# A tiled softmax on one core: the store of the first tile moves from Pool's DMA queue to SP's

## The chip, the core and the metric

The kernel runs on one core of one Trainium2 chip. The core has several engines, each with its own instruction stream: VectorE (DVE), ScalarE (ACT), GpSimd (POOL), SyncE (SP) and TensorE (PE, unused here). Data moves between the chip's memory and the core's on-chip memory by 16 DMA engines, which all DMA queues share. In this kernel three streams issue DMAs: SP, Pool and ACT. A DMA that one of them issues is cut into packets, and each of the 16 DMA engines moves a share of them.

The metric is the time of one execution in microseconds (us), as the device measures it. The changed kernel is compared with the kernel before.

## What is computed

The input `x` is a float32 array of 32 x 512 x 1024, 67.1 MB, and the temperature is 0.5. The output is the softmax over the last axis of `x / temperature`, in the same shape and type:

```python
def reference(x, temperature):
    scaled = x / temperature
    shifted = scaled - np.max(scaled, axis=-1, keepdims=True)
    exp_x = np.exp(shifted)
    return (exp_x / np.sum(exp_x, axis=-1, keepdims=True)).astype(np.float32)
```

All of `x` has to be read once and an output of the same size written once, 134.2 MB together.

## The kernel before

The 16,384 rows of 1024 numbers are cut into 11 tiles, which the code calls passes (`PASSES`, line 10). A tile has 128 partitions, and each partition holds 11, 12 or 9 whole rows: the first tile has 11 (5,632 KB), the next nine have 12 (6,144 KB each), the last has 9 (4,608 KB). Each tile is worked on in groups of rows, the numbers in `PASSES`: 4, 4 and 3 for the first tile, 6 and 6 for the next nine, 4, 3 and 2 for the last.

Only four tiles fit on chip at once (`BUFS = 4`, line 11). A tile is loaded, turned into its softmax in place and stored from the same buffer. Tile i + 4 reuses the buffer of tile i, so load i + 4 can't start before store i has landed.

For each group the work is:

- `maximum` (lines 63 to 72): DVE reduces each row to its maximum (line 69) and scales it into a bias (line 72).
- `exponential` (lines 74 to 85): ACT computes the exponential row by row, with that bias, and sums each row as it goes (line 78).
- `divide` (lines 87 to 98): DVE takes the reciprocal of the sums (line 90) and multiplies the rows by it, in one instruction for the group (line 93) or row by row (line 96).
- `store` (lines 100 to 109): after the last group of a tile, the whole tile is written with one DMA (line 108), and the load of the tile four further on is issued (line 60).

The order of instructions is written out by hand (`tc.manual_schedule()`, line 113): four loads first, then for each group its maximum and exponential, and after them the division and the store of the group before (near the end, for the first groups of the last two tiles, the division of the group before comes first). Each engine runs its own part of this order strictly in sequence, and waits where it needs another's result.

Three streams issue the DMAs:

- SP issues all loads (line 60), in the order of the tiles. From the fifth on, each waits for the store that frees its buffer.
- Pool issues the stores of tiles 0 to 5 (`BY_POOL = 6`, line 16). Its queue's descriptors are made by software; the profile calls the queue software_dynamic, q0.
- ACT issues the stores of tiles 6 to 10. The profile calls its queue hardware_dynamic, q10; SP's is hardware_dynamic too, q1.

Before the first store, Pool copies one number per partition out of tile 2 into a small tile named `seen` (line 106). The copy's result is not used. It makes Pool wait until tile 2 has been loaded, so that the store behind it on Pool's stream is not issued earlier.

The document calls the transfers load 0 to load 10 and store 0 to store 10, by tile.

Of the kernel before, what the change touches and what calls it, by code (L numbers as in the profile page):

```python
# [1 line left out]

# [4 lines left out]

PASSES = [[4, 4, 3]] + [[6, 6]] * 9 + [[4, 3, 2]]  # L10
BUFS = 4

WHOLE = (2, 3, 4, 6, 8)


BY_POOL = 6

ALONE = 9


@with_exitstack
def kernel(
    ctx: ExitStack,
    tc: tile.TileContext,
    x: bass.AP,
    temperature: bass.AP,
    out: bass.AP,
):
    nc = tc.nc
    f32 = mybir.dt.float32  # L30
    scale = 1.0 / float(temperature)
    extreme = mybir.AluOpType.max if scale > 0 else mybir.AluOpType.min

    P = 128
    xf = x.flatten_outer_dims()
    of = out.flatten_outer_dims()
    n, d = xf.shape
    rows = [sum(ks) for ks in PASSES]
    assert sum(rows) * P == n

    data = ctx.enter_context(tc.tile_pool(name="data", bufs=BUFS))
    stats = ctx.enter_context(tc.tile_pool(name="stats", bufs=4))


    groups = []
    for i, ks in enumerate(PASSES):
        for j, k in enumerate(ks):
            groups.append((i, sum(ks[:j]), k))

    def dram(t, i):  # L50
        block = t[P * sum(rows[:i]) : P * sum(rows[: i + 1]), :]
        return block.rearrange("(p k) d -> p k d", p=P, k=rows[i])

    tiles, small = [], []

    def load():
        i = len(tiles)
        if i < len(PASSES):
            xt = data.tile([P, rows[i], d], f32, name="xt")
            nc.sync.dma_start(out=xt, in_=dram(xf, i))  # L60
            tiles.append(xt)

    def maximum(g):
        i, a, k = groups[g]
        top, bias, sums, recip = (
            stats.tile([P, k], f32, name=name) for name in ("top", "bias", "sums", "recip")
        )
        small.append((bias, sums, recip))
        nc.vector.tensor_reduce(  # L69
            out=top, in_=tiles[i][:, a : a + k, :], axis=mybir.AxisListType.X, op=extreme  # L70
        )
        nc.vector.tensor_scalar_mul(bias, in0=top, scalar1=-scale)  # L72

    def exponential(g):
        i, a, k = groups[g]
        bias, sums, _ = small[g]
        for b in range(k):
            nc.scalar.activation(  # L78
                tiles[i][:, a + b, :],
                tiles[i][:, a + b, :],  # L80
                mybir.ActivationFunctionType.Exp,
                bias=bias[:, b : b + 1],
                scale=scale,
                accum_out=sums[:, b : b + 1],
            )

    def divide(g):
        i, a, k = groups[g]
        _, sums, recip = small[g]
        nc.vector.reciprocal(recip, sums)  # L90
        if i in WHOLE:
            xt = tiles[i][:, a : a + k, :]
            nc.vector.tensor_mul(xt, xt, recip.unsqueeze(2).to_broadcast([P, k, d]))  # L93
            return
        for b in range(k):
            nc.vector.tensor_scalar_mul(  # L96
                tiles[i][:, a + b, :], in0=tiles[i][:, a + b, :], scalar1=recip[:, b : b + 1]
            )

    def store(g):  # L100
        i, a, k = groups[g]
        if a + k == rows[i]:
            if i == 0:


                nc.gpsimd.tensor_copy(stats.tile([P, 1], f32, name="seen"), tiles[2][:, 0, 0:1])  # L106
            queue = nc.gpsimd if i < BY_POOL else nc.scalar
            queue.dma_start(out=dram(of, i), in_=tiles[i])  # L108
            load()

    with tc.manual_schedule():
        for _ in range(BUFS):
            load()
        for g in range(len(groups) + 1):

            alone = g < len(groups) and groups[g][0] >= ALONE and groups[g][1] == 0
            if g > 0 and alone:
                divide(g - 1)  # L120
                store(g - 1)
            if g < len(groups):
                maximum(g)
                exponential(g)
            if g > 0 and not alone:
                divide(g - 1)
                store(g - 1)


# [1 line left out]
_INS = ['x', 'temperature']  # L131
_OUTS = [((32, 512, 1024), 'float32')]

_NUMBERS = {'temperature': 0.5}


# [26 lines left out]
```

## Time and profile before

| | |
|---|---|
| Median of 3 runs | 317.3 us (317.12 to 318.05) |
| Span of the profiled execution | 316.0 us |
| DVE busy | 257.3 us, 81% of the span |
| ACT busy | 148.4 us, 47% |
| POOL busy | 3.7 us, 1% |
| Read from memory, written to it | 67.11 MB, 67.11 MB |
| Mean rate over the span | 425 GB/s |
| Issue to landing, stores by Pool, 6,144 KB | 36.6 us (median of 5) |
| Issue to landing, stores by ACT, 6,144 KB | 33.1 us (median of 4) |
| Issue to landing, loads by SP, 6,144 KB | 36.4 us (median of 9) |
| Issue to landing, store 0, by Pool, 5,632 KB | 29.2 us |
| Issue to landing, load 0, by SP, 5,632 KB | 15.6 us |

The profile is of one execution; its span runs from the first to the last recorded instruction or transfer, and times within it are counted from its start. The only time that the profile gives for that execution is its span. The runs' times are taken around the whole execution, and their median is 1.3 us longer.

"Issue to landing" is the time from the instruction that issues a DMA until its last byte has arrived. Transfers that are under way together share the 16 DMA engines, and one behind another in its queue waits for it, so these times are not the speed of one transfer.

The page also gives the chain of work that ended last, and the groups of instructions with what each waited for. A line such as "L69 DVE" means an instruction of line 69 on VectorE. A busy row has one digit for each of 40 equal slices of the span, in tenths; 9 is 90% or more.

### The profile page before, as it was taken

The numbers are of one execution on the slowest core, as the hardware profiler recorded it, in microseconds if no ns is written. First come the engines' busy times: TensorE is split into PE (matmuls) and PEld (weight loads), VectorE is DVE, ScalarE is ACT, GpSimd is POOL, SyncE is SP. The second block draws the span as 40 slices with busy tenths as digits, with TensorE's granted clock in tenths as the row PEclk, the third lists the DMA queues.
The fourth block names the chain that finished last, engine by engine and source line by source line (L and its number), as shares of the span: only waits on it lengthen the run. The fifth ranks groups of instructions, "written<-read, shape, count | busy, mean of one in ns | idle before, by whom it ended". The sixth has DMA issues, their size and how long they took to land.

```text
span 316.0 us, 529 instructions
## 1 busy us (share of the span) xinstructions
DVE 257.3 (81%) x150; ACT 148.4 (47%) x257; POOL 3.7 (1%) x11
## 2 busy tenths in 40 slices
DVE  0099999999999699979949993997399999888900
ACT  0048477468174444717181771447154705916600
POOL 0000010000000000000000000000000000000000
DMA  9999999999999999999999999999999999999995
GB/s 365 402 460 398 473 423 370 394 468 396 485 404 411 485 398 429 468 404 454 436 404 473 417 404 479 411 412 473 411 423 460 411 448 420 428 478 417 398 465 238
DMA packets 3171, 134.24 MB, mean 425 GB/s; under 512 B 352, under 2 KB 352, under 8 KB 352
## 3 DMA queue, kind: packets, MB, share of 16 engines
q1 hardware_dynamic: 1584, 67.11, 49.7%
q0 software_dynamic: 864, 37.22, 27.2%
q10 hardware_dynamic: 720, 29.88, 21.9%
q14 instruction: 3, 0.02, 0.0%
HBM read 67.11 MB, written 67.11 MB: 425 GB/s over the span
## 4 chain that ended last, share of the span: by engine, by line
DMA 47%; DVE 29%; ACT 10%; issue 9%; DVEq 0%; SPq 0%; POOLq 0%
DMA xt<-in_x_dram 24%; DMA out_dram<-xt 23%; DVE top L69 17%; ACT xt L78 10%; DVE xt L96 9%; DVE xt L93 2%; DVE bias L72 1%; DVE recip L90 0%; DVEq L158 0%; SPq L60 0%; POOLq L108 0%
## 5 line engine op out<-in xcount | busy, mean ns | idle before, releaser
L78 ACT ACTIVATE xt<-xt,bias 128x1024 f32<-128x1024 f32 x128 | 145.2, 1135 | 134.4 <-DVE recip L90 73.2
L69 DVE TENSOR_REDUCE top<-xt 128x6 f32<-128x6144 f32 (+3 forms) x24 | 140.1, 5836 | 36.9 <-DMA xt<-in_x_dram 36.9
L93 DVE TENSOR_TENSOR xt<-xt,recip 128x6144 f32<-128x6144 f32 x10 | 65.6, 6558 | 0.6 <-DVE recip L90 0.2
L96 DVE TENSOR_SCALAR xt<-xt,recip 128x1024 f32<-128x1024 f32 x68 | 46.3, 749 | 0.5
L78 ACT ACTIVATION_READ_ACCUMULATOR xt<-xt,bias 128x1 f32 x128 | 23.9, 186 | 0.0
L78 ACT ACT_TABLE_LOAD x1 | 1.3, 1283 | 16.4 <-DMA xt<-in_x_dram 16.4
L90 DVE RECIPROCAL recip<-sums 128x6 f32<-128x6 f32 (+3 forms) x24 | 4.3, 181 | 4.8 <-ACT xt L78 4.8
L108 POOL DMA_DIRECT2D out_dram<-xt x6 | 3.3, 555 | 128.9 <-ACT xt L78 83.7
L72 DVE TENSOR_SCALAR bias<-top 128x6 f32<-128x6 f32 (+3 forms) x24 | 4.1, 171 | 0.8
L106 POOL COPY seen<-xt 128x1 f32<-128x1 f32 x1 | 0.2, 185 | 45.0 <-DMA xt<-in_x_dram 45.0
L144 POOL MEMSET const-bfloat16-1.0<- 128x1 bf16 x1 | 0.1, 102 | 0.0
L144 POOL MEMSET const-uint8-127<- 128x1 uint8 x1 | 0.1, 102 | 0.0
L144 POOL MEMSET const-float32-0.0<- 128x1 f32 x1 | 0.1, 99 | 0.2 <-issue 0.2
L144 POOL MEMSET const-float32-1.0<- 128x1 f32 x1 | 0.1, 99 | 0.0
## 6 DMA issues: line engine op xcount, KB each, us to landing
xt<-in_x_dram SPq DMA_DIRECT2D x9, 6144.0 KB, 36.4
out_dram<-xt POOLq DMA_DIRECT2D x5, 6144.0 KB, 36.6
out_dram<-xt ACTq DMA_DIRECT2D x4, 6144.0 KB, 33.1
xt<-in_x_dram SPq DMA_DIRECT2D x1, 5632.0 KB, 15.6
out_dram<-xt POOLq DMA_DIRECT2D x1, 5632.0 KB, 29.2
xt<-in_x_dram SPq DMA_DIRECT2D x1, 4608.0 KB, 36.3
out_dram<-xt ACTq DMA_DIRECT2D x1, 4608.0 KB, 14.1
```

The source lines that it names most:

```text
L69: nc.vector.tensor_reduce(out=top, in_=tiles[i][:, a : a + k, :], axis=mybir.AxisListType.X, op=extreme)
L72: nc.vector.tensor_scalar_mul(bias, in0=top, scalar1=-scale)
L78: nc.scalar.activation(tiles[i][:, a + b, :], tiles[i][:, a + b, :], mybir.ActivationFunctionType.Exp, bias=bias[:, b : b + 1], scale=scal ...
L90: nc.vector.reciprocal(recip, sums)
L93: nc.vector.tensor_mul(xt, xt, recip.unsqueeze(2).to_broadcast([P, k, d]))
L96: nc.vector.tensor_scalar_mul(tiles[i][:, a + b, :], in0=tiles[i][:, a + b, :], scalar1=recip[:, b : b + 1])
L106: nc.gpsimd.tensor_copy(stats.tile([P, 1], f32, name="seen"), tiles[2][:, 0, 0:1])
L108: queue.dma_start(out=dram(of, i), in_=tiles[i])
L144: nc = _bacc.Bacc("TRN2", target_bir_lowering=False, num_devices=1)
```

## The change

One line decides which stream stores a tile. After the change the first tile's store is issued by SP instead of Pool. All other stores and all loads stay with their streams, and the copy into `seen` stays on Pool.

```diff
@@ -104,7 +104,7 @@
                 nc.gpsimd.tensor_copy(stats.tile([P, 1], f32, name="seen"), tiles[2][:, 0, 0:1])
-            queue = nc.gpsimd if i < BY_POOL else nc.scalar
+            queue = nc.sync if i == 0 else nc.gpsimd if i < BY_POOL else nc.scalar
             queue.dma_start(out=dram(of, i), in_=tiles[i])
             load()
```

On SP's stream the store stands behind loads 0 to 3 and ahead of load 4. On Pool's stream the first DMA is now store 1, and the copy into `seen` comes ahead of that. On DVE and ACT every instruction and its place are the same as before.

## The prediction

> **What bounds the kernel now.** I read the page first, its busy slices, its DMA queues and its chain.
>
> ```profile
> span 316.0 us, 529 instructions
> DVE  0099999999999699979949993997399999888900
> DMA  9999999999999999999999999999999999999995
> GB/s 365 402 460 398 473 423 370 394 468 396 485 404 411 485 398 429 468 404 454 436 404 473 417 404 479 411 412 473 411 423 460 411 448 420 428 478 417 398 465 238
> DMA packets 3171, 134.24 MB, mean 425 GB/s; under 512 B 352, under 2 KB 352, under 8 KB 352
> q1 hardware_dynamic: 1584, 67.11, 49.7%
> q0 software_dynamic: 864, 37.22, 27.2%
> q10 hardware_dynamic: 720, 29.88, 21.9%
> ```
>
> The DMA row is at 9 in every slice but the last, while VectorE (DVE) has holes. The kernel is bound by the 16 DMA engines: 134.24 MB in 316.0 us. (The slices' GB/s jump because a packet counts where it starts.) The three queues are SP's loads (q1), Pool's stores (q0) and ACT's stores (q10).
>
> Next I read the work by stretches: start and end, length, busy time of DVE, ACT and POOL, clock, DMA share, GB/s.
>
> ```profile
> 24.00:44.00 20.00, 19.61 (x21) 12.03 (x23) 0.00 (x0) 1.00 1.00 433
> 44.00:64.00 20.00, 19.86 (x16) 13.95 (x26) 0.85 (x2) 1.00 1.03 417
> 84.00:104.00 20.00, 19.86 (x8) 11.80 (x21) 0.53 (x1) 1.00 1.00 433
> 144.00:184.00 40.00, 35.14 (x24) 20.84 (x37) 1.07 (x2) 1.00 1.00 433
> 264.00:300.00 36.00, 31.33 (x34) 24.09 (x42) 0.00 (x0) 1.00 1.00 431
> ```
>
> The rate is 433 GB/s with loads alone (24 to 44), with SP and Pool sharing (84 to 184) and at the end, mostly with ACT alone. One stretch is lower, and cut to one microsecond it shows where:
>
> ```profile
> 48.00:49.00 1.00, 1.00 (x1) 0.58 (x2) 0.00 (x0) 1.00 3.09 786
> 49.00:50.00 1.00, 1.00 (x1) 0.00 (x0) 0.00 (x0) 1.00 0.00 0
> 50.00:51.00 1.00, 0.93 (x4) 0.41 (x1) 0.00 (x0) 1.00 0.00 0
> 51.00:52.00 1.00, 1.00 (x3) 1.00 (x3) 0.00 (x0) 1.00 1.56 676
> ```
>
> Sixteen packets, one to an engine, start between 48 and 49, and none again until after 51. In the trace's packet records a load packet (49,152 bytes) takes 1.815 us from the second tile on; these sixteen took 2.89 to 4.08. Summing packet bytes against the steady rate, the kernel is 2.50 us behind at 44 us (first load's start: first packet at 1.73, slow) and 3.78 us behind at 54, then between 3.63 and 3.79 until the end. So in the whole middle the DMA loses one thing: 1.27 us, just before the first store's packets. Pool's timeline names the neighbours:
>
> ```profile
> 45.46 0.18 POOL L106 COPY seen<-xt 128x1 f32<-128x1 f32 x1 [45.02 <-DMA xt<-in_x_dram]
> 46.04 0.67 POOL L108 DMA_DIRECT2D out_dram<-xt  x1 [0.39 <-issue]
> 65.86 0.53 POOL L108 DMA_DIRECT2D out_dram<-xt  x1 [19.16 <-DVE xt L96]
> ```
>
> Store 0 is issued at 46.04, 2.2 us ahead of the slow packets. It is at once the first store of the run and the first transfer of Pool's queue. That queue never runs empty later: each further store is issued before the one ahead of it has landed. ACT's queue starts at 208.8 and shows no such loss.
>
> **The change part by part.** The instructions are the same but for one: line 108's first DMA goes from Pool's queue to SP's, between load 3 and load 4. A 12-row tile is 8 packets per engine, 8 x 1.815 = 14.5 us alone; the 11-row first tile 8 x 1.665 = 13.3 us alone. Two busy queues alternate packet by packet, as the records from 53 to 69 us show.
>
> Removed: Pool's first DMA (0.67 us on Pool) and its wait behind the copy `seen`. Pool's next instruction, store 1, waits for DVE until 65.6 anyway, so nothing is gained there. As the first of its kind it may take 0.67 in place of 0.53; 0.13 us hidden under store 0's packets, and without that cover still 0.13.
>
> Added on SP: a wait for tile 0's last division (line 96, ends 43.84) and one DMA issue, 0.33 to 0.50 us by the load rows. Queued behind it on SP is load 4 alone, which waited for store 0's landing before too. Cost on SP nothing; the cover is load 3's packets.
>
> Store 0's own transfer: a store issued by SP is not in the trace. By the nearest rows, 45,056-byte packets take 1.665 us on q1 (load 0) and on q0 (store 0), and 49,152-byte ones 1.815 us on q1, q0 and ACT's hardware queue q10. I take the change at nothing; the bounds are in the stall below.
>
> The Trainium skill, in "DMA: Bandwidth & Descriptors" (Specifications and "Issuing engine by pattern"), says a simple store belongs on Sync, whose hardware path is generally faster, with about 0.6 us to the first byte against 1 us in software. Were that on the path, its 0.4 us would give an estimate of 316.9. Equal packet times on the queues above leave me at 317.3.
>
> Order: before, load 3 and store 0 shared the engines; store 0 landed at 46.04 + 29.2 = 75.24, load 3 at 71.4. Now store 0 stands behind load 3 in one ring; the rings keep order (loads 0, 1, 2 landed at 16.35, 30.87, 45.41, about 14.5 apart). Load 3 runs alone from 45.0 to 59.5, 11 us earlier, and gains nothing: DVE is busy until it reaches that tile at 78.9. Store 0 starts at 59.5. Store 1's first packet follows its issue at 65.86 by 1.0 us at the least (load 0: 0.74 to 1.73) and 6.3 at the most (ACT's first store: 208.80 to 215.07); I take 3.8 (load 4, issued at 75.31, first packet 79.08, one other queue busy, as here). So store 0 has the engines alone to 69.7, six of its eight packets; two alternate with store 1, 2 x 3.48 = 7.0, to 76.7, and it lands near 78, some 2.5 us later. Load 4 follows: before, it landed at 108.13; now between that and 111.5, the lower end if store 1 finishes before store 2's packets come. Store 1, which has the engines alone from 76.7 to 81.9, lands near 94 in place of 100.58.
>
> What is late next: pass 4's maximum by up to 3.4 us, and store 3 with it. None of it moves the end by itself, because bytes passed over are moved by the other queue: load 5 is issued when store 1 lands, near 94, some 14 us before load 4 ends (before: 100.64 against 108.13), so a next load always waits. The engines have no gap between 59.5 and the end. Cost 0.
>
> The tail decides whether that holds. Load 8 lands at 226.09 and DVE and ACT run from there to store 10's issue at 300.94; its first packet starts at 302.04, just as the first engine is done with store 9, and the last engine at 303.86. The slack is thus 0 to 1.8 us. Load 8's landing depends on how many store packets pass before it, so it can move by about one packet, 1.8 us, either way. Earlier is free; later costs 0 to 1.8. I take 0: when load 7 lands late, store 6 is issued late too and takes less from load 8.
>
> The stall: bounds -1.27 us (gone) and +1.27 (a second). I take 0: it comes with a queue's or a store's first start, and both still happen.
>
> The same skill page ("Latency and other measured facts") offers, as a best guess, that software descriptor rings load ports that some DMA engines need. The rows agree in part: at Pool's first store all 16 engines lost time, one 2.27 us, though later Pool stores cost none. By the guess the loss goes to Pool's first store wherever that is, an estimate of 317.3 again.
>
> Sum: span 316.0 + 0 (issue) + 0 (order) + 0 (tail) + 0 (stall) = 316.0; the median of the runs, 317.3, lies 1.3 us above the span, which I keep: 317.3 us.
>
> **The rivals.**
> *The stall disappears.* It may need loads and a newly started store queue side by side, or Pool's queue starting under full load traffic. Store 0 now follows load 3 in a running ring, and store 1 starts Pool's queue when only store 0 moves. For it: loads' packets were the slow ones, store 0's own were not, and ACT's first store cost nothing. Against: nothing shows that loads must be there. 317.3 - 1.27 = 316.0.
>
> *Pool's queue pays at each start from empty: slower.* Before, it started once. Now store 1 ends early: at 81.9 it has about three packets left, 3 x 3.63 = 10.9, so it ends near 92.8 and store 2 is issued at 92.89. The point is whether q0 is empty when store 2 arrives; if so, a second 1.27 us falls there: 318.6. For it: the sum puts both within 0.1 us. Against: SP's queue, empty from 71 to 79, and ACT's restarted without loss, and no row shows Pool's.
>
> *The tail idles: slower.* Load 8 lands a packet late, and store 10 is issued up to 1.8 us after the engines run dry: 317.3 + 0.9 to 1.8 = 318.2 to 319.1. Against it speaks the feedback above.
>
> **How the numbers follow.** Forecast, the stall moves or stays: 0.46, 317.3, own range 317.1 to 318.05 (the runs shown). Stall gone: 0.29. Second start: 0.14. Tail: 0.11. No run can tell less than 0.3% (0.95 us) from no change; 1.27 us is over it. So faster 0.29, same 0.46, slower 0.25. The range runs from the lowest run less the stall, 317.12 - 1.27 = 315.85, rounded to 315.8, to 318.7, just over the second start; the far half of the tail's case is left out.
>
> **What would show it.** Right: load 3 landing near 60, store 0 near 78, load 4 at 108 to 111.5, a stretch of 433 GB/s from 45 to 65, and one run of long packets near 66 to 70 (or at 60, if it belongs to the first store). No long packets: first rival. Another group near 93 to 97: second. Store 10's first packet more than 1.1 us behind the end of store 9's: third. I am wrong altogether if a store in SP's queue moves at another rate than 433 GB/s, or if load 5 is issued after load 4 has landed.

## The result, and the profile after

| | before | after |
|---|---|---|
| Median of 4 runs each | 317.31 us (317.12 to 318.05) | 328.24 us (327.62 to 329.63) |
| Ratio, after to before | | 1.034 (95% interval 1.0312 to 1.0369) |
| Span of the profiled execution | 316.0 us | 325.9 us |
| Store 10 issued | 300.94 us | 310.13 us |
| Last packet ended | 314.7 us | 324.3 us |

The change costs 10.9 us by the medians and 9.9 us by the profiled spans. The prediction, no change, was wrong, and its range did not hold the time. The page after, the same lines as before:

```profile
span 325.9 us, 528 instructions
DVE  0099999999999049999979990599599999878900
DMA  9999999999699999999999999999999999999995
GB/s 354 444 392 471 398 465 404 362 451 475 290 380 392 440 428 440 428 363 392 386 380 398 392 452 416 452 411 458 404 458 410 422 418 458 431 418 452 416 430 240
DMA packets 3171, 134.24 MB, mean 412 GB/s; under 512 B 352, under 2 KB 352, under 8 KB 352
q1 hardware_dynamic: 1728, 72.88, 53.8%
q0 software_dynamic: 720, 31.46, 23.0%
q10 hardware_dynamic: 720, 29.88, 21.2%
```

Store 0's 5.77 MB went from q0 to q1, as the change says, and the bytes are the same. New is a 6 in the DMA row, in the eleventh slice (81 to 90 us), with 290 GB/s in the row below. Further on, slices 18 to 23 (139 to 187 us) have DMA at 9 throughout and yet only 363 to 398 GB/s: the engines are busy and move less. The work by stretches (start and end, length, busy time of DVE, ACT and POOL, clock, DMA share, GB/s) puts both in numbers, and the short ones show two places closely:

```profile
24.00:44.00 20.00, 19.61 (x20) 12.03 (x21) 0.00 (x0) 1.00 1.00 433
44.00:64.00 20.00, 19.86 (x17) 13.94 (x25) 0.18 (x1) 1.00 1.01 414
84.00:104.00 20.00, 19.86 (x8) 11.47 (x21) 0.53 (x1) 1.00 0.92 354
144.00:184.00 40.00, 38.03 (x24) 21.07 (x39) 1.06 (x2) 1.00 0.98 379
264.00:300.00 36.00, 32.37 (x23) 17.73 (x31) 0.00 (x0) 1.00 1.00 434
...
57.00:58.00 1.00, 1.00 (x1) 0.83 (x2) 0.00 (x0) 1.00 2.78 786
58.00:59.00 1.00, 1.00 (x1) 0.00 (x0) 0.00 (x0) 1.00 0.00 0
59.00:60.00 1.00, 1.00 (x1) 0.00 (x0) 0.00 (x0) 1.00 0.00 0
60.00:61.00 1.00, 1.00 (x1) 0.00 (x0) 0.00 (x0) 1.00 1.67 721
...
88.00:89.00 1.00, 1.00 (x1) 1.00 (x3) 0.00 (x0) 1.00 0.01 0
89.00:90.00 1.00, 1.00 (x1) 1.00 (x3) 0.00 (x0) 1.00 0.16 49
90.00:91.00 1.00, 1.00 (x1) 1.00 (x3) 0.00 (x0) 1.00 2.42 737
```

From 84 to 104 the rate fell from 433 to 354 GB/s, and near 89 the engines stood empty. From 144 to 184 it fell from 433 to 379 with a DMA share of 0.98: the packets took longer. The loss at the first store is still there, at 57 to 61 in place of 48 to 52.

The prediction's own measure was packet bytes against the steady 433 GB/s. By it the 9.6 us between the last packets' ends come as follows:

| stretch | lost more than before |
|---|---|
| first store's start (45 to 55 before, 55 to 65 after) | -0.3 us |
| 85 to 100 us | +3.9 us |
| 140 to 185 us | +5.2 us |
| everything else, in small parts | +0.8 us, what is left |

The chain of waits names what emptied the engines (start and length in us, what). First before, then after:

```profile
65.86 34.72 DMA out_dram<-xt
100.58 0.02 SPq L60
...
100.64 22.04 DMA xt<-in_x_dram
```

```profile
66.20 22.79 DMA out_dram<-xt
88.98 0.02 SPq L60
89.01 0.03 issue
89.04 29.19 DMA xt<-in_x_dram
118.22 0.02 issue
118.25 6.56 DVE top L69
```

The transfer that begins at 66.20 is store 1, and what it releases at 88.98 is SP. SP's timeline after (start, length, instruction, count) says which loads those are:

```profile
0.74 1.88 SPq L60 DMA_DIRECT2D xt<-in_x_dram  x4
44.20 0.34 SPq L108 DMA_DIRECT2D out_dram<-xt  x1
89.04 38.92 SPq L60 DMA_DIRECT2D xt<-in_x_dram  x3
```

Behind four loads and store 0, the next instruction is load 4, at 89.04. Store 0 had landed at 79.94, so load 4 was not released by store 0. The list of waits of the built programs, which the prediction did not read, says it outright (semaphore names: DMASW0 is Pool's first DMA, DMASW1 its second, DMAHW0 to DMAHW4 the first to fifth DMA of a hardware queue; "xt_129" is load 4, "xt_170" load 5):

```
before
5 L60 DMACopy xt_129<-in_x_dram 128x12288 [waits DMAHW0_49,DMASW0_49,DVE_49]
6 L60 DMACopy xt_170<-in_x_dram 128x12288 [waits DMAHW1_49,DMASW1_49,DVE_49]
after
5 L108 DMACopy out_0_dram<-xt_63 128x11264 [waits DMAHW0_49,DVE_49]
6 L60 DMACopy xt_129<-in_x_dram 128x12288 [waits DMAHW1_49,DMASW0_49,DVE_49]
7 L60 DMACopy xt_170<-in_x_dram 128x12288 [waits DMAHW4_49]
```

Before, load 4 waits for load 0's and store 0's end: it takes tile 0's buffer, and load 5 takes tile 1's. After, load 4 waits for load 1 and for Pool's first DMA, which is now store 1: it takes tile 1's buffer, and load 5, behind it, waits for store 0 and takes tile 0's. The order of the instructions is the predicted one; the tile pool, which hands out the four buffers, gave two of them the other way round. The later tiles follow in turn: tile 8 takes tile 4's buffer, tile 9 tile 5's.

### The profile page after: what moved, and what is told of

Its sections match the earlier page's. It is cut to its first block, busy times and chain, and to the rows that moved or that the text cites. A ratio compares the mean times of both kernels' runs of the same rounds, so it can differ in the third digit from the quotient of the medians.

```text
span 325.9 us, 528 instructions
## 1 busy us (share of the span) xinstructions
DVE 257.2 (79%) x150; ACT 148.4 (46%) x257; POOL 3.2 (1%) x10
## 4 chain that ended last, share of the span: by engine, by line
DMA 44%; DVE 32%; ACT 10%; issue 8%; DVEq 0%; SPq 0%; POOLq 0%
DMA xt<-in_x_dram 26%; DVE top L69 19%; DMA out_dram<-xt 19%; ACT xt L78 10%; DVE xt L96 8%; DVE xt L93 4%; DVE bias L72 1%; DVE recip L90 1%; DVEq L158 0%; SPq L60 0%; POOLq L108 0%
## 5 line engine op out<-in xcount | busy, mean ns | idle before, releaser
L96 DVE TENSOR_SCALAR xt<-xt,recip 128x1024 f32<-128x1024 f32 x68 | 46.3, 747 | 0.5
L108 POOL DMA_DIRECT2D out_dram<-xt x5 | 2.8, 558 | 134.2 <-ACT xt L78 91.2
```

The lines of the kernel that those rows point to most:

```text
L96: nc.vector.tensor_scalar_mul(tiles[i][:, a + b, :], in0=tiles[i][:, a + b, :], scalar1=recip[:, b : b + 1])
```

## Experiments

The first question is whether the buffers or the queue cost the time. Three others came up on the way: whether a store among the loads costs something of its own, what made the packets long from 140 to 185 us, and why moving the store with the old buffers still left 2.3 us. In the recorded texts the letters stand for these: A, the swapped buffers make the loss; P, the order of load and store packets on an engine makes packets long; K, the engines drift apart while two stores alternate; L, load 4 is merely issued late.

### Which buffer, or which queue

Two kernels give tile i buffer i modulo 4 by four pools of one buffer each. The first is the changed kernel, the second the kernel before with the same edit, as a control:

```diff
-    data = ctx.enter_context(tc.tile_pool(name="data", bufs=BUFS))
+    data = [
+        ctx.enter_context(tc.tile_pool(name=f"data{b}", bufs=1)) for b in range(BUFS)
+    ]
...
-            xt = data.tile([P, rows[i], d], f32, name="xt")
+            xt = data[i % BUFS].tile([P, rows[i], d], f32, name="xt")
```

> Store 0 stays on SP, but each tile has a buffer of its own turn (tile i in buffer i mod 4), so load 4 waits for store 0 and load 5 for store 1. Theory A (the loss comes from the swapped buffers, by which load 4 waits for store 1): load 4 is issued near 80 in place of 89, the engines never run dry, 317.3 within 1 us. Theory B (a store in the queue of the loads costs by itself, wherever the buffers are): still 326 to 329.

> The kernel before, with four pools of one buffer each in place of one pool of four; store 0 by Pool. A and B alike: 317.3 within 0.5 us, with load 4 issued near 75. If it differs, the four pools cost something themselves, and the other runs are to be read against this one.

The third leaves store 0 on Pool and swaps the buffers alone, for tiles 4 and 5 and for 8 and 9, which follow them:

```diff
-            xt = data[i % BUFS].tile([P, rows[i], d], f32, name="xt")
+            xt = data[(i ^ 1 if i in (4, 5, 8, 9) else i) % BUFS].tile([P, rows[i], d], f32, name="xt")
```

> Store 0 by Pool as before the change; tiles 4 and 8 take the second buffer and tiles 5 and 9 the first, so load 4 waits for store 1. Theory A: load 4 is issued when store 1 lands, near 89 to 100, the engines run dry before it or shortly after, and the time is 326 to 330. Theory B: 317.3 within 1 us. In between would say that both take part.

| | median (lowest to highest) | ratio to before |
|---|---|---|
| store 0 on SP, buffers in turn | 319.64 us (317.64 to 320.66) | 1.0066 (1.0046 to 1.0085) |
| store 0 on Pool, buffers in turn | 317.32 us (316.95 to 319.53) | 1.0003 (0.9978 to 1.0029) |
| store 0 on Pool, buffers swapped | 328.07 us (327.62 to 328.86) | 1.0343 (1.0322 to 1.0364) |

The third kernel and its control came out as theory A said; the first missed both ranges, by 1.3 us above A's and far below B's. Swapped buffers alone make the whole loss, with store 0 still on Pool. Its stretches and its chain are those of the changed kernel:

```profile
84.00:104.00 20.00, 19.86 (x8) 11.30 (x19) 0.53 (x1) 1.00 0.92 354
144.00:184.00 40.00, 38.83 (x24) 21.89 (x39) 1.07 (x2) 1.00 0.98 377
```

```profile
66.37 22.63 DMA out_dram<-xt
...
89.07 29.52 DMA xt<-in_x_dram
```

With the store on SP and the buffers in turn, both stretches are whole again:

```profile
84.00:104.00 20.00, 19.86 (x8) 11.35 (x19) 0.53 (x1) 1.00 1.00 433
144.00:184.00 40.00, 35.10 (x23) 20.70 (x36) 1.07 (x2) 1.00 1.00 435
```

So 8.6 of the 10.9 us (328.24 - 319.64) go with the buffers. Another 2.3 us (319.64 - 317.31) stay with the store on SP, which neither stretch shows. The two don't add up: the swap alone cost 10.7 us, the store on SP alone 2.3, and both together 10.9. In the changed kernel store 0's engines ended 2.4 us apart, but store 1's only 0.6, at 88.0 to 88.6, just before the engines ran dry.

### What a store in the loads' queue costs by itself

To see whether the 2.3 us belong to SP's queue, store 0 went to ACT's, buffers in turn:

```diff
-            queue = nc.sync if i == 0 else nc.gpsimd if i < BY_POOL else nc.scalar
+            queue = nc.scalar if i == 0 or i >= BY_POOL else nc.gpsimd
```

> Buffers in turn as in the first of these runs, store 0 by ACT, whose queue no other store uses until store 6. Theory A: 317.3 within 1 us, since the buffers alone decide. Theory B (cost of the loads' queue): 317.3 too. A third theory, that the loss at the first store belongs to Pool's queue, expects 316.0 here if ACT's queue starts without loss; the trace of the changed kernel speaks against it, as there the slow packets came ahead of SP's store: 1.0 to 1.3 us are lost again.

It took 322.22 us (319.51 to 323.59), ratio 1.0145 (1.0094 to 1.0197): slower than on SP, and a miss for all three theories. Its stretches near the end show the loss:

```profile
285.00:300.00 15.00, 13.65 (x14) 6.53 (x11) 0.00 (x0) 1.00 0.87 374
300.00:315.00 15.00, 7.19 (x11) 3.88 (x8) 0.00 (x0) 1.00 0.72 311
```

In the kernel before, the same stretches have 419 and 370 GB/s. The packet records tell why. Each of the 16 DMA engines brings its own share of a transfer, and by its end there is a first engine and a last one. The table has the end of the first and of the last engine's share, in us. A transfer lands behind the last: before, load 8 landed at 226.09.

| | store 0 | load 8 | load 10 | last transfer |
|---|---|---|---|---|
| before | 73.6 to 74.9 | 224.1 to 225.7 | 278.5 to 280.3 | 313.0 to 314.7 |
| the change | 77.1 to 79.5 | 224.3 to 235.0 | 285.3 to 289.8 | 321.9 to 324.3 |
| on SP, buffers in turn | 77.0 to 80.1 | 222.1 to 225.9 | 276.5 to 281.8 | 312.9 to 316.3 |
| on ACT, buffers in turn | 76.7 to 79.1 | 218.3 to 232.5 | 275.4 to 287.5 | 319.4 to 320.2 |

On ACT's queue the engines drifted 14.2 us apart by load 8. Those ahead ran out of work near the end, while DVE waited for the share of those behind. On SP's queue the drift is 3 us from store 0 on, and it comes out as a last transfer whose engines end 3.4 us apart. By packet bytes against the steady rate, that kernel was 0.16 us behind the kernel before at 45 us and still 0.16 at 310, so its loss is in the last transfers. That gave a theory, K: the engines drift apart while store 0's and store 1's packets alternate, and the drift costs the time. Its rival, L, was that load 4 is issued late (80.6 against 75.3). Two edits held store 1 back by copies on Pool, one by a little (1 copy), one until store 0 is nearly through (4 copies):

```diff
+            if i == 1:
+                junk = junks.tile([P, 1024], f32, name="junk")
+                for _ in range(4):
+                    nc.gpsimd.tensor_copy(junk, tiles[i][:, rows[i] - 1, 0:1024])
```

> Store 0 by SP, buffers in turn (319.6 so far), with one copy of a row on Pool ahead of store 1, about 1 us. Theory K (the remaining 2.3 us come from the engines drifting apart, which starts when store 1's first packet meets some engines just before and others just after a packet's end, and a transfer lands with its last engine): another start moves the spread, and the time changes by 1 to 3 us either way, with the end following the spread of the last transfers. Rival L (store 0's later landing costs the 2.3 us): 319.6 within 0.5 us, whatever the spread is.

> Store 0 by SP, buffers in turn (319.6), with four copies of a row on Pool ahead of store 1, so that store 1's packets start when store 0's are done and the two never alternate. Theory K: no engine meets store 1 earlier than another in the middle of store 0, the spread stays under 2 us, store 0 lands near 74.5, and the time is 317.0 to 317.8. Theory L expects 317.3 too, since store 0 lands early. If a store in the loads' queue costs something by itself, it stays at 319.6.

With 1 copy store 1 was issued at 67.0 and the time stayed: 319.49 us (319.13 to 320.2), ratio 1.0064 (1.0041 to 1.0086), with store 0's engines again 3.0 us apart. The change that K expected did not come, and the time stayed as L said; but the spread had not changed either, so the run doesn't separate the two. With 4 copies store 1 was issued at 70.07, store 0's engines ended within 73.4 to 74.1, no transfer was ever more than 1.2 us apart, and the median was 317.24 us (nine of the twelve runs from 317.03 to 318.11, three from 319.96 to 322.03), ratio 1.0013 (0.998 to 1.0045). Its stretches:

```profile
84.00:104.00 20.00, 19.86 (x8) 11.63 (x21) 0.53 (x1) 1.00 1.00 433
144.00:184.00 40.00, 35.10 (x23) 20.91 (x37) 1.06 (x2) 1.00 1.00 433
```

So a store in the loads' queue need not cost anything that can be measured, and it brought nothing either: no kernel of this study is faster than the one before.

Load 4 was also earlier there (74.5), so L was not yet out. Two kernels with store 0 on Pool and buffers in turn issued load 4 late by itself, behind copies on Pool that read tile 0. The first kernel had 13 copies of 1024 numbers per partition, the second these:

```diff
+            if i == 1:
+                junk = junks.tile([P, 1024], f32, name="junk")
+                for n in [1024] * 7 + [64]:
+                    nc.gpsimd.tensor_copy(junk[:, 0:n], tiles[0][:, 0, 0:n])
+                load()
+            if i > 0:
+                load()
```

> Store 0 by Pool, buffers in turn (317.3 so far), but load 4 is held until Pool has made 13 copies of a row behind store 1's issue, so that it is issued near 80 in place of 75, as late as where SP stores tile 0. Theory L (the later load 4 costs the 2.3 us by which SP's store of tile 0 with buffers in turn is slower): 319 to 320. Theory K (the engines' drifting apart costs them, and being late by itself is made up by the other queue): 317.3 within 0.8 us, if the spread between the first and the last engine of a transfer stays near 1 to 2 us; slower only if that spread grows.

> As the run in which load 4 is held behind copies on Pool, but with eight copies, the last one short, so that load 4 is issued near 80 and not at 87.5, and the engines don't run dry. Store 0 by Pool, buffers in turn (317.3 without the copies). Theory L (a later load 4 costs the 2.3 us by itself): 319 to 320. Theory K (what costs is the spread between the first and the last engine of a transfer): 317.3 within 0.8 us if the spread stays below 2 us, and up to 320 if it reaches 3 us or more.

With 13 full copies load 4 came at 87.5, later than meant, and the engines ran nearly dry: 321.59 us (319.1 to 323.45), ratio 1.0118 (1.0075 to 1.0161), of which 2.4 us were lost from 85 to 105, and its engines then drifted up to 5.1 us apart. That is another loss than the one in question, both expectations missed, and nothing follows. With 8 copies load 4 came at 81.0, as late as with the store on SP, the engines stayed within 2.1 us, and the time was 317.51 us (316.93 to 319.55), ratio 1.0001 (0.9979 to 1.0023). L falls: a late load 4 by itself costs nothing that can be told. K stands in so far as the 2.3 us went where the drift went. What makes the engines drift isn't shown. That two stores alternate can't be all of it: on ACT's queue store 0 ran beside load 3 first, and the drift grew from 2.4 us there to 14.2 at load 8.

### What made the packets long

From 140 to 185 us of the changed kernel the engines are busy, and a 49,152-byte packet of load 6 or store 3 takes 2.07 or 2.06 us on average, against 1.815. The records don't name the engine of a packet, but packets follow one another closely enough to be strung together. Fifteen of the 16 strings put each load packet ahead of the store packet of the same number, and in most of these pairs one of the two, more often the store's, takes 2.1 to 3.4 us, typically 2.4. In the sixteenth the store is one packet ahead, and all but two of its packets stay at 1.81. Theory P: the order decides, a load's packet with the store's packet of the same place in the transfer behind it. Store 3 was held back by 3, 1 and 2 copies on Pool in the changed kernel:

```diff
+            if i == 3:
+                junk = junks.tile([P, 1024], f32, name="junk")
+                for _ in range(3):
+                    nc.gpsimd.tensor_copy(junk, tiles[i][:, rows[i] - 1, 0:1024])
```

> The changed kernel (store 0 on SP, buffers swapped), with three copies of one row on Pool between tile 3's last division and store 3, so that store 3 starts some us behind load 6 in place of together with it. Theory P (in the changed kernel the 5 us between 140 and 190 are lost because load 6 and store 3 move the same packet numbers side by side, load packet k and then store packet k on each engine): their packets go back to 1.815 us, and 322 to 324.5 remain of 328.2. Rival S (the loss comes from the engines being out of step, or from this stretch as such): 327 to 330.

> The changed kernel with one copy ahead of store 3 (three made 323.8 of 328.2). Theory P in its bare form: if store 3's first packet still comes right behind load 6's first on most engines, the packets beside it stay long and the time is 327 to 329; if it comes a packet later, they are 1.815 us and the time is 323 to 324.5. A rival by which the delay helps in proportion (1 us of 3): about 326.7 whatever the order.

> The same with two copies. Theory P: again one of two times by the order of the first packets, 327 to 329 or 323 to 324.5, and 323 to 324.5 the likelier, as store 3 is issued some 2 us later than in the changed kernel. The rival in proportion: about 325.3.

| copies | store 3 issued | engines with long packets | median | ratio to before |
|---|---|---|---|---|
| 0 (the change) | 132.2 | 15 | 328.24 us | 1.034 (1.0312 to 1.0369) |
| 1 | 133.7 | nearly all | 328.18 us (326.92 to 329.29) | 1.0324 (1.0286 to 1.0361) |
| 2 | 134.2 | 4 | 328.54 us (327.45 to 330.11) | 1.0344 (1.0299 to 1.039) |
| 3 | 135.3 | none | 323.79 us (323.23 to 324.57) | 1.0197 (1.016 to 1.0233) |

With 3 copies, 3.1 us of delay bring 4.5 us back: that stretch is whole and the first loss stays.

```profile
84.00:104.00 20.00, 19.86 (x8) 11.41 (x20) 0.53 (x1) 1.00 0.91 354
144.00:184.00 40.00, 39.79 (x24) 22.32 (x40) 1.07 (x2) 1.00 1.00 431
```

With 2 copies both orders are in one execution. These are two of its strings from 136 us on, L for load 6, S for store 3, with the time of each packet in us:

```
engine A   L1.81 L1.81 S1.81 L1.81 S1.81 L1.81 S1.81 L1.81 S1.81 L1.81 S1.81
engine B   L1.81 S1.81 L1.81 S2.40 L1.81 S2.48 L1.81 S2.44 L1.81 S2.45 L1.81
```

Engine A had two load packets before the store's first, engine B one. They run at the same moments, and only B's store packets are long. Twelve engines went like A, four like B. So the long packets go with the order on each engine, not with the moment. But the time did not fall, and its expectation, 323 to 324.5, missed. Twelve engines were now ahead of four: load 6 ended on them between 162.8 and 169.0, load 8 between 222.7 and 237.1, and those ahead idled at the end, by the stretches:

```profile
144.00:184.00 40.00, 39.79 (x24) 22.31 (x40) 1.06 (x2) 1.00 1.00 420
285.00:300.00 15.00, 12.43 (x13) 6.11 (x11) 0.00 (x0) 1.00 0.86 373
300.00:315.00 15.00, 10.55 (x16) 8.55 (x16) 0.00 (x0) 1.00 0.79 338
```

The middle stretch is nearly whole (420 GB/s) and the tail has what it saved: a loss on four engines cost as much as one on fifteen.

A sharper form of P was that packets of the same place, and so the same partitions, disturb each other. Two kernels wrote store 3 as two DMAs, partitions 64 to 127 first, meant to make the places differ, and then 0 to 63 first as a control:

```diff
-            queue.dma_start(out=dram(of, i), in_=tiles[i])
+            if i == 3:
+                for half in (slice(64, 128), slice(0, 64)):
+                    queue.dma_start(out=dram(of, i)[half], in_=tiles[i][half])
+            else:
+                queue.dma_start(out=dram(of, i), in_=tiles[i])
```

> The changed kernel with store 3 in two transfers, partitions 64 to 127 first and then 0 to 63, so that the store moves the other half of the partitions than the load beside it. Theory P: the long packets between 136 and 169 are gone, 322 to 324.5. Rival S: 327 to 330.

> The control to the run with halves: the changed kernel with store 3 in two transfers, partitions 0 to 63 first. Theory P: the store's first half meets the load's packets of the same partitions on half of the engines only, so 324 to 328, slower than with the upper half first. Rival S: the same as with the upper half first, both 327 to 330. If both are near 323, the second transfer or the other share of partitions per engine is what helps, not the order.

They took 331.53 us (329.25 to 333.07), ratio 1.0433 (1.0372 to 1.0494), and 333.14 us (331.13 to 335.08), ratio 1.0489 (1.0433 to 1.0546), with packets of up to 4.6 us in the first. Both are slower than the change and beyond what P or its rival S had said. So the sharper form has no support, and the order of the halves does not help. As the records don't say which partitions a packet holds, and a store in two parts changes more than the places, they don't rule it out.

The last one tried to bring the slow order about in the kernel before, with buffers in turn, by 7 such copies ahead of store 3:

> Store 0 by Pool, buffers in turn (317.3), with seven copies of a row on Pool ahead of store 3, so that its first packet should follow load 6's first packet on most engines, as in the changed kernel. Theory P in its bare form (a store that starts right behind the first packet of a load, and goes on packet by packet beside it, is slow together with that load): packets of 2 us and more between 131 and 160, and 320 to 324. Rival (the slow packets of the changed kernel need something else of that kernel): packets of 1.815 us and 317.3 to 318.5. If the start misses the step, the trace shows it and nothing follows.

It took 318.1 us (317.34 to 319.17), ratio 1.0017 (0.9995 to 1.0039). Store 3's packets came ahead of load 6's, so the slow order was not reached, and nothing follows.

## Why the prediction was wrong, by its own steps

**What bounds the kernel: right.** The engines' bytes and losses account for the time after as for the time before.

**The step that failed: load 4 behind store 0.** The prediction said "Queued behind it on SP is load 4 alone, which waited for store 0's landing before too", and then "Load 4 follows". It took which store a load waits for from the kernel before, and compared only the order of instructions, in which nothing else moved. In the changed program load 4 waits for store 1. Shown by the waits listed above, by load 4's issue at 89.04, 9.1 us after store 0's landing, and by the kernel that swaps the buffers alone: 328.07 us. The prediction's two signs of being "wrong altogether" missed this: load 5 was issued at 89.42, long before load 4 landed at 118.22, and the store on SP's queue moved at the steady rate (from 65 to 75 us it lost 0.03 us). Its line "load 4 at 108 to 111.5" was the one that showed it.

**"The engines have no gap between 59.5 and the end. Cost 0": wrong as its consequence.** It rested on load 4 being under way when store 1 lands, with load 5 following, near 94. With loads 4 and 5 both behind store 1, nothing was left to move at 88.6. What it costs by 100 us is 3.9 us: empty engines from 88.6 to 90.0, slow first packets of load 4 (1.9 to 3.4 us), and a loss of about 1.2 us near 96 to 99 as store 2 joins the loads. The further 5.2 us, long packets from 140 to 185, had no term in the sum. They came with the shifted order of load and store packets, and 3 us of delay at one store takes them away; why the order matters is open.

**Load 3 and store 0 themselves: right.** Load 3's last packet ended at 60.8 (said: near 60), store 0's at 79.5 (near 78). Store 1 landed at 88.98 (near 94), earlier because load 4 was not there to share with.

**Pool's and SP's instructions cost nothing: right.** With buffers in turn and store 1 held back, the store on SP costs nothing that can be told (1.0013).

**The stall: taken at 0, and right.** The loss moved from 48 to 52 us to 57 to 61, with store 0, and measures 1.0 in place of 1.3 us. None appears at Pool's first DMA, store 1 at 66.20. So it goes with the first store behind loads and not with Pool's queue. Its size is not fixed: with store 0 on ACT's queue it was 0.5 us. The Trainium skill ("DMA: Bandwidth & Descriptors", "Latency and other measured facts") offers contention by the software queues' descriptor rings as its best guess at why two of the 16 engines are usually slower. The prediction stretched that to this loss and said that by it the loss would go to Pool's first store; it stayed with a store on SP, so the guess does not explain it here. The rival "the stall disappears" is out with it.

**"Pool's queue pays at each start from empty": not borne out as such.** A second loss, about 1.2 us, did come near 96, about where the rival said (93 to 97), when store 2 reached Pool's empty queue and joined load 4. It came with the swapped buffers, both with store 0 on SP and with it on Pool, and with buffers in turn only in the kernel with 13 copies, whose engines had also run nearly dry. But starts from empty without it are on record: Pool's first, store 1 at 66.20; store 3 at 135.27 in the changed kernel with 3 copies, after store 2 had landed at 127.59; and store 2 at 94.78 in the kernel with 8 copies, after store 1 had landed at 94.57. What this loss needs is open.

**"The tail idles": the wrong place in the change, but a true mechanism.** In the changed kernel the tail added well under 1 us: its engines were up to 12.5 us apart at store 5, but only 2.4 at the last transfer. In the kernels on ACT's queue and with 2 copies it lost some 5 us, because the engines had drifted 14 us apart. The prediction took the 16 engines as one, with a slack of 0 to 1.8 us, and had no term for their drift. (Its packet at 302.04 was store 9's last; store 10's first started at 302.09, which changes nothing.) With buffers in turn, the change as meant would have cost 2.3 us by that, which also lies outside its range of 315.8 to 318.7.

**What stays open.** Why the tile pool gave the buffers the other way round when a store changed its queue was not tried. The built programs hold one hint: in their lists of all DMAs store 0 stands ahead of store 1 before the change and behind it after, so the buffers may be handed out in the order in which the builder takes them to come free. Nor is it known why a store's packet takes 2.45 us in the one order and 1.81 in the other, what causes the loss at the first store, what pulls the engines apart, and when a drift closes again.

## What to carry to other kernels

An edit that changes which queue does something can change which buffer a later tile gets: compare the waits of the built program, not only its order, and give buffers out by hand where a load's wait matters. Where a loop keeps the DMA engines full, ask for each load which transfer it waits for and whether another is under way at that moment; two loads behind one store made a hole here. And where the DMA share stayed near 1 at a lower rate (0.98 at 379 GB/s), the packets had grown long: look at the packets by engine, and at the first and last engine's end, before the mean.

## What the hardware showed that was not expected

- The 16 DMA engines do not stay in step. In kernels of 317 us the shares of a transfer end 0.4 to 2.1 us apart; with store 0 on SP and buffers in turn up to 5.3; in the changed kernel up to 12.5; at the worst 15.1, with 2 copies. The Trainium skill says in "DMA: Bandwidth & Descriptors" ("Queues, rings and completion order") that each engine takes turns between its queues packet by packet on its own. The alternating strings agree; that the engines then drift apart is what these runs add.
- A 49,152-byte packet took 1.815 us on each of the three queues, but about 2.45 in one order of loads and stores, on some engines and not on others at the same time.
- A copy of 128 x 1024 float32 on Pool took 1.04 us, but 6.44 when it was issued during DVE's multiplication of a whole group, and that was for 64 numbers per partition. DVE's timeline of the kernel with 8 copies (start, length, line, operation; its edits move the line numbers, and L96 is the multiplication of a whole group), where that copy runs from 74.5 to 81.0:

```profile
72.44 0.94 DVE L75 TENSOR_SCALAR bias<-top 128x6 f32<-128x6 f32 x1
...
73.58 7.29 DVE L96 TENSOR_TENSOR xt<-xt,recip 128x6144 f32<-128x6144 f32 x1
...
87.66 6.56 DVE L96 TENSOR_TENSOR xt<-xt,recip 128x6144 f32<-128x6144 f32 x1
```

The copy ended just behind DVE's instruction (80.87), and DVE itself took 7.29 in place of 6.56 us there, and 0.94 in place of 0.17 on the small one that overlapped the copies before. "SBUF — State Buffer" in the same skill says that an instruction of DVE with two inputs on chip and a reading one of Pool exclude each other; the row of the multiplication agrees. The small instruction, with one such input, is not covered by that sentence. This wait is also why load 4 came later than meant in the kernel with 13 copies: one of its copies took 7.25 us in the same place.
